# Two-layer decoder trunk: split-precision gate and numerator products, the last gate chunk by DRAM, and the order of some lanes

## The chip, the cores and the metric

The kernel runs on one core of one Trainium2 chip. The metric is the device time of one launch in microseconds (us). The kernel before took 1051.79 us in the median of three runs (1050.85 to 1053.89).

## The reference, cut to what matters

Batch 1, 256 positions (T), width 2048 (D), two layers. All weights and activations are float32.

```python
# even layer: HGRN2 (a) and RG-LRU (b) side by side
u = rmsnorm(h) @ e_w_in                     # qa, fa, ia, za, xb, zb
ya = head_rmsnorm(hgrn2(qa, fa, ia)) * silu(za)
xc = causal_conv(xb)
r  = sigmoid(einsum('bsnc,ncd->bsnd', xc, b_w_r) + b_b_r)   # 8 blocks of 128 x 128
ig = sigmoid(einsum('bsnc,ncd->bsnd', xc, b_w_i) + b_b_i)
yb = linear_scan(a(r), sqrt(1 - a*a) * ig * xc) * silu(zb)
h += concat(ya, yb) @ e_w_out
# odd layer: mLSTM, 8 heads, keys of 128, values of 256
u = rmsnorm(h) @ o_w_in                     # q, k, v, og, z, ig, fg
sc  = (q @ k.T) * weights_from_gates        # causal, so 3 of 4 blocks of 128 x 128
num = sc @ v ; den = sc.sum(-1)
yc  = head_rmsnorm(num / max(|den|, exp(-m))) * sigmoid(og) * silu(z)
h += yc @ o_w_out
# after each layer
pl = rmsnorm(p[i] @ ple_w[i]) ; h = h + sigmoid(h @ ple_gate_w[i]) * pl
return rmsnorm(h)
```

## The kernel before

**Split products.** A float32 product is made of three matmuls of a rounded type (fp32r). Each weight tile of 128 x 1024 is loaded by SP as `raw` (5 buffers), copied by ScalarE to `whi` (L131) and its remainder subtracted by VectorE into `wlo` (L132); both have four buffers, a buffer being free again once TensorE's last matmul on it is done. Activations are split the same way by `split_act` (L145, L146) into tiles `ahl` (12 buffers). `mm3` (L150 to L152) issues the three products hi-hi, hi-lo and lo-hi into one PSUM accumulator. Some smaller products are instead a float32 matmul, which the trace records as two passes: the gates of the RG-LRU (L823), the scores (L1058, L1059) and numerators (L1070, L1072) of the mLSTM, the gate sums (L929), the spread of the log weights (L265), the transposes of L542.

**Large projections.** `block` (L161: 16 matmuls of 512 columns, L167: 16 of 256) makes feature-major results, `quarter_tok` (L225, L226, L227) token-major ones: one quarter of the contraction is 24 matmuls of 512 columns, and `project_tok` makes 512 output columns of four quarters. `chunks` makes pairs of outputs in the order (0, quarters 0 to 2), (1, quarters 0 to 2), (0, 3), (1, 3), so that the last part of `y` may come later. L338 is the small per-layer embedding, L1194 to L1196 the final gate's 256-column products.

**Order.** Everything that isn't a large projection lives in generators, the lanes: `rg` (RG-LRU), `att` (HGRN2), `qk`, `mix` (mLSTM), `fm0` to `fm3` (gate output to feature-major), `emb`. `pump()` in the middle of a quarter, or between the two halves of a `block`, takes one step of some lanes, and a `yield` in a lane ends a step; so a lane's matmuls stand between two matmuls of a projection, and a `yield` more or less moves them by one pump. `drain(...)` runs a lane to its end at once. Within this, the scheduler puts each engine's instructions into one fixed order; each engine then works its list in that order and waits on semaphores for the others.

**What the change touches.** `rg_lru` holds two halves r of four blocks each: weights `bw` (128 x 1024, two gates), inputs `xc` (128 x 1024); its gates are 8 float32 matmuls per half, in two groups. `mix(j)` works on two heads: it spreads the log weights (L265), exponentiates them into `wt`, multiplies the scores by them into `scw` (L1060), and sums numerators (6 float32 matmuls per j, 257 columns: 256 values and a column of ones for the denominator); `vt` holds the values, written by ScalarE from PSUM (L1101). A `mix(j)` is started after value chunk j. `feature_major` transposes 32 x 32 blocks on VectorE, writes to DRAM through POOL's queue and reads back (`across`: one write, L507, and four reads, L510, `lag` pumps later); `feature_major_pe` does it with eight TensorE transposes of 128 x 128 (L542) for the last gate chunk (fm3), since the output projection needs it at once: `drain("fm0", ..., "fm3")` stands before `out_proj`. `gate_sums` (L929) adds four matmuls with 32 output rows per chunk c of the first layer's final gate, used for the second layer's input and forget gates.

Of the kernel before, what the change touches and what calls it, by code (L numbers as in the profile page):

```python
# [43 lines left out]
def trunk(ctx: ExitStack, tc: tile.TileContext, a, out):  # L44
# [365 lines left out]
                step(f"{lane}{kq}")  # L410
        return before

    def out_proj(hq, w, y, lane):

        act = {}
        for c in range(4):
            ps = project_tok(w, c, y)
            with tc.high_priority(offset=100):
                for hf in range(2):
                    v.tensor_tensor(out=hq[c][:, hf], in0=ps[hf], in1=hq[c][:, hf], op=ALU.add)  # L420
            start(f"{lane}{c}", to_features(hq[c], c, act, None, lane))
            step(f"{lane}{c}")
        return act
# [88 lines left out]
        for _ in range(lag):  # L512
            yield

    def feature_major(u, gain, first, y, room):

        w = room("w")
        w5 = w.rearrange("p (j c h t) -> p h c j t", j=4, c=4, h=2)
        for hf in range(2):
            v.transpose(w5[:, hf], u[:, hf].rearrange("p (c j q) -> p c j q", c=4, j=4))  # L520
        r = room("r")
        yield from across(w, r, f"du{gain}{first}", 5)
        r5 = r.rearrange("p (i c h t) -> p c h i t", i=4, c=4, h=2)
        for b in range(2):
            x = tp.tile([P, 512], F32, name="xr", tag="hn", bufs=3)
            for k in range(2):
                s.activation(x[:, k * T:(k + 1) * T].rearrange("p (h i t) -> p h i t", h=2, i=4), r5[:, 2 * b + k],
                             AF.Copy, scale=pc(gain, first + 2 * b + k))
            y[first // 2 + b] = split_act(x, "y")

    def feature_major_pe(u, gain, first, y):

        yield
        yield
        banks = []
        for b in range(2):
            ps = px.tile([P, 512], F32, name="mx", tag="mx")
            for k in range(2):
                c = (2 * b + k) * P
                for hf in range(2):  # L540
                    o = k * T + hf * P
                    te.transpose(ps[:, o:o + P], u[:, hf, c:c + P], ident)  # L542
            banks.append(ps)
        yield
        for b, ps in enumerate(banks):
            hi, lo, both = act_pair()
            for k in range(2):
                scaled_split(ps[:, k * T:(k + 1) * T], gain, first + 2 * b + k, hi[:, k], lo[:, k])
            y[first // 2 + b] = (hi, lo, both)

    def gate_tok(w, j, act, u):

# [52 lines left out]
    with m0_scope:  # L605
# [203 lines left out]
        def rg_lru(r, xc):  # L809
            bw = m0.tile([P, 2, 512], F32, name="bw", tag="bw", bufs=1)  # L810
            sy.dma_start(out=bw, in_=a["bw"][r])
            av = m0.tile([P, 1024], F32, name="av", tag="f")
            tt = m0.tile([P, 1024], F32, name="tt", tag="k")
            it = m0.tile([P, 1024], F32, name="it", tag="it", bufs=1)
            yield
            if r:
                yield
            for j in range(2):
                for w, (dst, bias) in enumerate(((av, "bbr"), (it, "bbi"))):
                    ps = px.tile([P, 512], F32, name="mx", tag="mx")  # L820
                    for i in range(2):
                        c = 2 * j + i
                        te.matmul(ps[:, i * T:(i + 1) * T], bw[:, w, c * P:(c + 1) * P], xc[:, c * T:(c + 1) * T],  # L823
                                  start=True, stop=True)
# [18 lines left out]
            v.tensor_tensor(out=it, in0=it, in1=tt, op=ALU.mult)  # L843
# [80 lines left out]
    v.tensor_tensor(out=wt[:, :, 0:16], in0=gr, in1=pall("on").unsqueeze(2).to_broadcast([P, KT, 16]), op=ALU.mult)  # L924
    gps = px.tile([P, 512], F32, name="mx", tag="mx")

    def gate_sums(c, r5):
        for x in range(4):
            te.matmul(gps[32 * x:32 * x + 32, 0:T].rearrange("p (h i t) -> p h i t", h=2, i=4), wt[:, 4 * c + x],  # L929
                      r5[:, x], start=(c == 0), stop=(c == 3))  # L930

    acth = ple_gate(hq, a["g0"], act, pls, rp0, hss0, "on", "fg", ready(act, "fe"), gate_sums)
    l0.close()
# [14 lines left out]
    with tc.tile_pool(name="m1", bufs=2) as m1:  # L948
# [89 lines left out]
        def mix(j):  # L1038
# [12 lines left out]
                s.activation(wt[:, i, T:384], wt[:, i, T:384], AF.Exp, bias=aT[:, 8 + hd:9 + hd])  # L1051
            yield
            yield
            scw = room("scw")[:, 0:768].rearrange("p (i t) -> p i t", i=2)
            for i in range(2):
                q, k = qk[j][:, i * T:(i + 1) * T], qk[4 + j][:, i * T:(i + 1) * T]
                sc = px.tile([P, 512], F32, name="mx", tag="mx")
                te.matmul(sc[:, 0:T], k[:, 0:P], q, start=True, stop=True)  # L1058
                te.matmul(sc[:, T:384], k[:, P:T], q[:, P:T], start=True, stop=True)  # L1059
                v.scalar_tensor_tensor(scw[:, i, :], sc[:, 0:384], SC, wt[:, i, :], op0=ALU.mult, op1=ALU.mult)  # L1060
            yield

            vt = vts[j]
            nm = m1.tile([P, 2, 512], F32, name="num", tag="vt", bufs=6)
            for i in range(2):
                pool, tag = ((px, "mx"), (pst, "st"))[i]
                for hf in range(2):
                    c = hf * 8 + 2 * j + i
                    ps = pool.tile([P, 512], F32, name="nu", tag=tag)[:, 0:VW]
                    te.matmul(ps, scw[:, i, hf * P:(hf + 1) * P], vt[:, 0, i], start=True, stop=(hf == 0))  # L1070
                    if hf:
                        te.matmul(ps, scw[:, i, T:384], vt[:, 1, i], start=False, stop=True)  # L1072
                    o = nm[:, hf, i * 256:(i + 1) * 256]
                    s.copy(o, ps[:, 0:256])
                    v.tensor_copy(den[:, c:c + 1], ps[:, 256:VW])
# [19 lines left out]

        for j in range(4):
            psv = project_tok(a["ov"], j, acth)
            vt = m1.tile([P, 2, 2, VW], F32, name="vt", tag="vt", bufs=6)
            gp.memset(vt[:, :, :, 256:VW], 1.0)
            for hf in range(2):  # L1100
                s.activation(vt[:, hf, :, 0:256], psv[hf].rearrange("p (i e) -> p i e", i=2), AF.Copy,  # L1101
                             scale=norm["rt"][:, hf:hf + 1])
# [19 lines left out]
        for j in range(4):  # L1122
            u = m1.tile([P, 2, 512], F32, name="u", tag="vt", bufs=6)
            gate_tok(a["oz"], j, acth, u)
            for hf in range(2):
                for i in range(2):
# [234 lines left out]
```

## Time and profile before

| | |
|---|---|
| median of three runs | 1051.79 us |
| the profiled execution | 1051.14 us |
| its span | 1049.4 us |
| TensorE (PE) busy | 1038.6 us, 99% |
| VectorE (DVE) busy | 724.3 us, 69% |
| ScalarE (ACT) busy | 594.3 us, 57% |
| GpSimd (POOL) busy | 114.4 us, 11% |
| granted TensorE clock | 0.998 |
| DMA | 225.40 MB, mean 215 GB/s |

The profile is one execution. PE's busy time counts overlapped instructions once. Matmuls are pipelined: the "mean ns of one" in a group of matmuls is from its start to its modelled end and overlaps with the next one's, so the cost of one in a stream is read from the chain of waits, whose pieces give a start and the time until the next piece starts. Where a piece says "x8", 8 records lie in it; a float32 matmul leaves two records.

### The profile page before, as it was taken

To read this page: it belongs to the slowest core of one execution; us is meant where nothing else is said; L and a number is where in the kernel's file an instruction comes from. 1 tells how busy PE (TensorE), PEld (TensorE's weight loads), DVE (VectorE), ACT (ScalarE), POOL (GpSimd) and SP (SyncE) were. 2 spreads that over 40 slices of the span, in tenths; PEclk is the share of its full clock that TensorE was granted. 3 is DMA by queue.
4 is the path that set the end of the run, shared out by engine and by line. 5 is a ranking of instruction groups with operands and counts; after the bars stand their busy time and mean duration, and the time that the engine had idled before them with its cause. 6 is when DMAs were issued, how large, how long until landed. Compare 5 with 4: busy or idle time off the path is not lost.

```text
span 1049.4 us, 14961 instructions
## 1 busy us (share of the span) xinstructions
PE 1038.6 (99%) x5504; PEld 869.1 (83%) x5504; DVE 724.3 (69%) x1085; ACT 594.3 (57%) x893; POOL 114.4 (11%) x162
## 2 busy tenths in 40 slices
PE   9999999999999999999999999999999999999996
PEld 7888888888888888887888788888888888888886
DVE  6857897997877666766569864454457767666675
ACT  7775545869654444565557765544445565444553
POOL 0001232522201111111021000000001110111000
PEclk9999999999999999999999999999999999999999
DMA  9865544545867877687597644446557775977652
GB/s 350 311 205 192 172 164 157 182 150 192 275 234 258 249 247 230 212 277 235 177 271 248 203 169 160 161 161 201 199 188 225 250 262 187 294 239 242 201 181 81
DMA packets 64587, 225.40 MB, mean 215 GB/s; under 512 B 8065, under 2 KB 9345, under 8 KB 64513
## 3 DMA queue, kind: packets, MB, share of 16 engines
q1 hardware_dynamic: 55440, 196.38, 56.5%
q0 software_dynamic: 8496, 27.27, 8.6%
q8 instruction: 43, 0.70, 0.3%
q10 hardware_dynamic: 576, 0.79, 0.2%
q14 instruction: 32, 0.25, 0.1%
HBM read 211.30 MB, written 13.11 MB: 214 GB/s over the span
## 4 chain that ended last, share of the span: by engine, by line
PE 97%; DMA 1%; ACT 1%; DVE 0%; issue 0%; SPq 0%; ACTq 0%
PE mm L225 22%; PE mm L226 22%; PE mm L227 22%; PE mm L161 11%; PE mm L167 6%; PE mx L225 2%; PE mx L227 2%; PE mx L226 2%; PE mm L338 1%; DMA xq<-in_xT_dram 1%; PE mm L1196 1%; PE mm L1195 1%; PE mm L1194 1%; PE mx L823 1%; PE nu L1070 1%; PE mx L661 0%
## 5 line engine op out<-in xcount | busy, mean ns | idle before, releaser
L132 DVE TENSOR_TENSOR wlo<-raw,whi 128x1024 fp32r<-128x1024 f32 (+1 forms) x364 | 439.9, 1220 | 246.4 <-ACT whi L131 211.3
L131 ACT CAST whi<-raw 128x1024 fp32r<-128x1024 f32 (+1 forms) x364 | 378.3, 1043 | 356.4 <-PE mm L227 254.8
L225 PE MATMUL mm<-whi,ahl 128*128 128x512 f32 x1024 | 401.5, 392 | 0.0
L227 PE MATMUL mm<-whi,ahl 128*128 128x512 f32 x1024 | 398.5, 389 | 0.0
L226 PE MATMUL mm<-wlo,ahl 128*128 128x512 f32 x1024 | 398.4, 389 | 0.0
L225 PEld LDWEIGHTS mm<-whi,ahl 128*128 128x128 f32 x1024 | 192.2, 188 | 42.0 <-issue 2.1
L227 PEld LDWEIGHTS mm<-whi,ahl 128*128 128x128 f32 x1024 | 192.2, 188 | 40.5
L226 PEld LDWEIGHTS mm<-wlo,ahl 128*128 128x128 f32 x1024 | 192.3, 188 | 39.8 <-DVE wlo L132 0.5
L161 PE MATMUL mm<-ahl,whi 128*128 128x512 f32 x512 | 122.1, 390 | 0.0
L161 PEld LDWEIGHTS mm<-ahl,whi 128*128 128x128 f32 x512 | 94.2, 188 | 18.3
L167 PE MATMUL mm<-ahl,wlo 128*128 128x256 f32 x512 | 67.7, 285 | 0.0
L167 PEld LDWEIGHTS mm<-ahl,wlo 128*128 128x128 f32 x512 | 64.9, 191 | 2.2
L225 PE MATMUL mx<-whi,ahl 128*128 128x512 f32 x96 | 37.5, 391 | 0.0
L227 PE MATMUL mx<-whi,ahl 128*128 128x512 f32 x96 | 37.4, 389 | 0.0
L226 PE MATMUL mx<-wlo,ahl 128*128 128x512 f32 x96 | 37.3, 389 | 0.0
L507 POOL DMA_DIRECT2D ducn<-w x3 | 1.7, 561 | 206.2 <-DVE w L520 206.2
L173 ACT COPY sm<-mm 128x256 f32<-128x256 f32 x32 | 11.7, 366 | 19.1 <-PE mm L167 19.0
L225 PEld LDWEIGHTS mx<-whi,ahl 128*128 128x128 f32 x96 | 18.0, 188 | 3.7
L227 PEld LDWEIGHTS mx<-whi,ahl 128*128 128x128 f32 x96 | 18.0, 188 | 3.8
L226 PEld LDWEIGHTS mx<-wlo,ahl 128*128 128x128 f32 x96 | 18.0, 188 | 3.7
L971 DVE SCALAR_TENSOR_TENSOR qk<-xr,prm,qk 128x255 f32<-128x255 f32 (+2 forms) x48 | 20.4, 475 | 0.6 <-ACT qk L968 0.5
L1195 PE MATMUL mm<-wlo,ahl 128*128 128x256 f32 x64 | 18.1, 283 | 0.0
(304 smaller groups left out, 877.3 us busy)
## 6 DMA issues: line engine op xcount, KB each, us to landing
raw<-in_ew_dram SPq DMA_DIRECT2D x64, 512.0 KB, 4.4
raw<-in_g_dram SPq DMA_DIRECT2D x56, 512.0 KB, 4.7
raw<-in_eo_dram SPq DMA_DIRECT2D x32, 512.0 KB, 4.8
raw<-in_oqk_dram SPq DMA_DIRECT2D x32, 512.0 KB, 4.6
raw<-in_ov_dram SPq DMA_DIRECT2D x32, 512.0 KB, 3.8
raw<-in_oog_dram SPq DMA_DIRECT2D x32, 512.0 KB, 3.7
raw<-in_oz_dram SPq DMA_DIRECT2D x32, 512.0 KB, 4.2
raw<-in_oo_dram SPq DMA_DIRECT2D x32, 512.0 KB, 4.5
```

The lines of the kernel that those rows point to most:

```text
L131: last["act"] = s.copy(h, r).ins
L132: last["dve"] = v.tensor_tensor(out=l, in0=r, in1=h.bitcast(F32), op=ALU.subtract).ins
L161: last["pe"] = te.matmul(ps, parts[k // 8][0][:, c:c + P], act[k // 2][2][:, (k % 2) * 512:(k % 2 + 1) * 512], start=(k == 0), stop=False).ins
L167: last["pe"] = te.matmul(ps[:, T:2 * T], parts[k // 8][1][:, c:c + P], act[k // 2][0][:, k % 2], start=False, stop=(k == KT - 1)).ins
L173: s.copy(small, ps[:, T:2 * T])
L225: te.matmul(ps[hf], xh, wh, start=(k == 0), stop=False)
L226: te.matmul(ps[hf], xh, wl, start=False, stop=False)
L227: last["pe"] = te.matmul(ps[hf], xl, wh, start=False, stop=(k == KT - 1)).ins
L338: last["pe"] = te.matmul(ps[hf], tokens(pact[x], k, hf), (hi, lo)[y][:, k * 512:(k + 1) * 512], start=(n == mine[0]), stop=(n == mine[-1]) ...
L823: te.matmul(ps[:, i * T:(i + 1) * T], bw[:, w, c * P:(c + 1) * P], xc[:, c * T:(c + 1) * T], start=True, stop=True)
L971: v.scalar_tensor_tensor(dst[:, sh:T], pi[:, 0:T - sh], pc("ccw", k * 16 + n), dst[:, sh:T], op0=ALU.mult, op1=ALU.add)
L1195: te.matmul(ps[hf], xh, wl, start=False, stop=False)
```

## The change

It has six edits.

1. The RG-LRU's gates become three products each. `bw` is split into a `whi` and a `wlo` buffer of the weights' own pools, `xc` into two `ahl` tiles. One step is added ahead of the gates.
2. The numerators become three products each. The scores are written over `wt`, split into `sh` and `sl`; the values' remainder `vl` is an `ahl` tile. The value tile has 258 columns instead of 257.
3. The last gate chunk goes by VectorE transposes and DRAM like the other three; `feature_major_pe` is gone. `out_proj` takes its chunks from a generator, and the second one draws from `chunks` and waits for the `fm` lanes as it needs them.
4. The first layer's mixer outputs (`fm` of "an") start their transposes one step later, with a lag of 4 instead of 5.
5. All four `mix(j)` are started behind value chunk 0, each waits for its keys and values by steps, and the step after the numerators is gone, so that the next pair's spread stands right behind them.
6. `gate_sums` collects two chunks and issues eight matmuls at once, twice instead of four groups of four.

```diff
-    def out_proj(hq, w, y, lane):
+    def out_proj(hq, parts, lane):
         act = {}
-        for c in range(4):
-            ps = project_tok(w, c, y)
+        for c, ps in enumerate(parts):
...
-    def feature_major(u, gain, first, y, room):
-
+    def feature_major(u, gain, first, y, room, lag):
+
+        if lag < 5:
+            yield
         w = room("w")
         w5 = w.rearrange("p (j c h t) -> p h c j t", j=4, c=4, h=2)
         for hf in range(2):
             v.transpose(w5[:, hf], u[:, hf].rearrange("p (c j q) -> p c j q", c=4, j=4))
         r = room("r")
-        yield from across(w, r, f"du{gain}{first}", 5)
+        yield from across(w, r, f"du{gain}{first}", lag)
...
-    def feature_major_pe(u, gain, first, y):
-
-        yield
-        yield
-        banks = []
-        for b in range(2):
-            ps = px.tile([P, 512], F32, name="mx", tag="mx")
-            for k in range(2):
-                c = (2 * b + k) * P
-                for hf in range(2):
-                    o = k * T + hf * P
-                    te.transpose(ps[:, o:o + P], u[:, hf, c:c + P], ident)
-            banks.append(ps)
...
@@ rg_lru
             yield
             if r:
                 yield
+            bh, bl = (wp.tile([P, 2, 512], F32R, name=n, tag=n) for n in ("whi", "wlo"))
+            s.copy(bh, bw)
+            v.tensor_tensor(out=bl, in0=bw, in1=bh.bitcast(F32), op=ALU.subtract)
+            xs = [split_act(xc[:, j * 512:(j + 1) * 512], "xc") for j in range(2)]
+            yield
             for j in range(2):
                 for w, (dst, bias) in enumerate(((av, "bbr"), (it, "bbi"))):
                     ps = px.tile([P, 512], F32, name="mx", tag="mx")
                     for i in range(2):
                         c = 2 * j + i
-                        te.matmul(ps[:, i * T:(i + 1) * T], bw[:, w, c * P:(c + 1) * P], xc[:, c * T:(c + 1) * T],
-                                  start=True, stop=True)
+                        mm3(ps[:, i * T:(i + 1) * T], bh[:, w, c * P:(c + 1) * P], bl[:, w, c * P:(c + 1) * P], xs[j], i,
+                            True, True)
...
-                start(f"fm{g}", feature_major(u, "an", 4 * g, y, room0))
+                start(f"fm{g}", feature_major(u, "an", 4 * g, y, room0, 4))
...
-    act = out_proj(hq, a["eo"], y, "fe")
+    act = out_proj(hq, (project_tok(a["eo"], c, y) for c in range(4)), "fe")
...
+    held5 = []
+
     def gate_sums(c, r5):
-        for x in range(4):
-            te.matmul(gps[32 * x:32 * x + 32, 0:T].rearrange("p (h i t) -> p h i t", h=2, i=4), wt[:, 4 * c + x],
-                      r5[:, x], start=(c == 0), stop=(c == 3))
+        held5.append((c, r5))
+        if c % 2 == 0:
+            return
+        for n, r in held5:
+            for x in range(4):
+                te.matmul(gps[32 * x:32 * x + 32, 0:T].rearrange("p (h i t) -> p h i t", h=2, i=4), wt[:, 4 * n + x],
+                          r[:, x], start=(n == 0), stop=(n == 3))
+        held5.clear()
...
-        VW = 257
+        VW = 258
...
@@ mix(j)
             yield
             yield
-            scw = room("scw")[:, 0:768].rearrange("p (i t) -> p i t", i=2)
+            while 4 + j not in qk:
+                yield
             for i in range(2):
...
-                v.scalar_tensor_tensor(scw[:, i, :], sc[:, 0:384], SC, wt[:, i, :], op0=ALU.mult, op1=ALU.mult)
-            yield
-
-            vt = vts[j]
+                v.scalar_tensor_tensor(wt[:, i, :], sc[:, 0:384], SC, wt[:, i, :], op0=ALU.mult, op1=ALU.mult)
+            sh, sl = (bp.tile([P, 1024], F32R, name=n, tag="wt")[:, 0:768].rearrange("p (i t) -> p i t", i=2)
+                      for n in ("sh", "sl"))
+            s.copy(sh, wt)
+            v.tensor_tensor(out=sl, in0=wt, in1=sh.bitcast(F32), op=ALU.subtract)
+            yield
+
+            while len(vts) <= j:
+                yield
+            vh, vl = vts[j]
...
-                    te.matmul(ps, scw[:, i, hf * P:(hf + 1) * P], vt[:, 0, i], start=True, stop=(hf == 0))
-                    if hf:
-                        te.matmul(ps, scw[:, i, T:384], vt[:, 1, i], start=False, stop=True)
+                    for b, o in ((0, hf * P), (1, T))[:1 + hf]:
+                        for x, y, n in ((sh, vh, VW), (sl, vh, VW), (sh, vl, T)):
+                            te.matmul(ps[:, 0:n], x[:, i, o:o + P], y[:, b, i], start=(b == 0 and x is sh and y is vh),
+                                      stop=(b == hf and y is vl))
...
             nums[j] = nm
-            yield
...
         for j in range(4):
             psv = project_tok(a["ov"], j, acth)
-            vt = m1.tile([P, 2, 2, VW], F32, name="vt", tag="vt", bufs=6)
-            gp.memset(vt[:, :, :, 256:VW], 1.0)
+            vt = m1.tile([P, 2, 2, VW], F32R, name="vt", tag="vt", bufs=6)
+            gp.memset(vt.bitcast(F32)[:, :, :, 256:VW], 1.0)
+            vl = ap.tile([P, 1024], F32R, name="vl", tag="ahl").rearrange("p (h i e) -> p h i e", h=2, i=2)
             for hf in range(2):
...
+                v.scalar_tensor_tensor(vl[:, hf], src, norm["rt"][:, hf:hf + 1], vt[:, hf, :, 0:256].bitcast(F32),
+                                       op0=ALU.mult, op1=ALU.subtract)
+            vts.append((vt, vl))
+            if j == 0:
+                drain("qk0", "qk2")
+                for c in range(4):
+                    start("mix", mix(c))
+                start("mix", mix_norm())
-            vts.append(vt)
-            for c in (j // 2, 2 + j // 2):
-                drain(f"qk{c}")
-            start("mix", mix(j))
-        start("mix", mix_norm())
...
-            start(f"fm{j}", feature_major(u, "cn", 4 * j, y, room) if j < 3 else feature_major_pe(u, "cn", 4 * j, y))
+            start(f"fm{j}", feature_major(u, "cn", 4 * j, y, room, 5))
...
-        drain("fm0", "fm1", "fm2", "fm3")
+        step("fm3")
         start("emb", embed_norm())
-        act = out_proj(hq, a["oo"], y, "fo")
+        act = out_proj(hq, chunks(a["oo"], 4, y, ready(y, "fm")), "fo")
```

What it does to the order, first on TensorE around the numerators of a head pair (nu; L1070 and L1072 before, L1072 in the changed file). Before:

```order
L226 MATMUL mm<-wlo,ahl 128x512
L227 MATMUL mm<-whi,ahl 128x512
L1070 MATMUL nu<-vt,scw 128x257 x2
L1072 MATMUL nu<-vt,scw 128x257
L1070 MATMUL nu<-vt,scw 128x257 x2
L1072 MATMUL nu<-vt,scw 128x257
L225 MATMUL mm<-whi,ahl 128x512
```

In the change, the end of the same group:

```order
L1072 MATMUL nu<-vl,sh 128x256
L1072 MATMUL nu<-vt,sh 128x258
L1072 MATMUL nu<-vt,sl 128x258
L1072 MATMUL nu<-vl,sh 128x256
L265 MATMUL mx<-s_5670,identr 128x256 x2
L225 MATMUL mm<-whi,ahl 128x512
```

A group of 6 matmuls (12 recorded passes) becomes one of 18, and the next pair's spread (L265, of the split log weights s), which came one pump of 24 matmuls later before, stands right behind it.

On ScalarE, around the gates of the second RG-LRU half (av and it are the gates' sigmoids, o the HGRN2 output copied from PSUM, sq its squares, u a gate chunk). Before:

```order
L827 ACTIVATE av<-mx,prm 128x256 x2
L827 ACTIVATE it<-mx,prm 128x256 x2
L131 CAST whi<-raw 128x1024 x2
L556 ACTIVATE u<-mm,rth 128x512
L833 ACTIVATE tt<-av,sp_235 128x256 x2
L834 ACT_TABLE_LOAD
L834 ACTIVATE av<-av,spm_236 128x256
L787 COPY o<-mx 128x512
L790 ACTIVATE sq,hss<-mx 128x128 x4
L787 COPY o<-mx 128x512
L790 ACTIVATE sq,hss<-mx 128x128 x4
L827 ACT_TABLE_LOAD
```

In the change:

```order
L800 CAST whi<-bw 128x1024
L145 CAST ahl<-xc 128x2x256
L131 CAST whi<-raw 128x1024
L537 ACTIVATE u<-mm,rth 128x512
L768 COPY o<-mx 128x512
L771 ACTIVATE sq,hss<-mx 128x128 x4
L768 COPY o<-mx 128x512
L771 ACTIVATE sq,hss<-mx 128x128 x4
L131 CAST whi<-raw 128x1024 x2
L813 ACT_TABLE_LOAD
L813 ACTIVATE av<-mx,prm 128x256 x2
```

The copy of bw into a `whi` buffer (L800) and the second split of xc (L145) are added, and the first sigmoids have moved behind the squares. Before, both weight copies of the coming quarter (L131 x2) stood ahead of the squares; now one does, and the other is the first of the two behind them.

On VectorE at the same place, in the change:

```order
L801 TENSOR_TENSOR wlo<-bw,whi 128x1024
L132 TENSOR_TENSOR wlo<-raw,whi 128x1024
L538 SCALAR_TENSOR_TENSOR u<-u,mm 128x512
L146 TENSOR_TENSOR ahl<-xc,ahl 128x2x256
L872 TENSOR_TENSOR u<-u,o 128x512
L772 TENSOR_SCALAR hss<-hss 128x8
L232 TENSOR_SCALAR hnt<-hss 128x8
L234 TENSOR_SCALAR hny<-hss 128x8
L233 TENSOR_SCALAR hnr<-hnt 128x8
L236 TENSOR_TENSOR hnt<-hnr 128x8
L237 TENSOR_TENSOR hnt<-hnt,hny 128x8
L238 SCALAR_TENSOR_TENSOR hnr<-hnt,hnr 128x8
L132 TENSOR_TENSOR wlo<-raw,whi 128x1024
```

The subtraction for `bl` (L801), the remainder of xc (L146) and seven small operations of the reciprocal root on 128x8 stand ahead of the weights' subtraction L132 in the last row; before, both weight subtractions of that quarter stood ahead of all the small ones, between the operations on the two halves of u.

More of the change, by code (lines that the diff above doesn't have):

```diff
@@ L529, in feature_major @@
             y[first // 2 + b] = split_act(x, "y")
-    def feature_major_pe(u, gain, first, y):
-        yield
-        yield
-        banks = []
-        for b in range(2):
-            ps = px.tile([P, 512], F32, name="mx", tag="mx")
-            for k in range(2):
-                c = (2 * b + k) * P
-                for hf in range(2):
-                    o = k * T + hf * P
-                    te.transpose(ps[:, o:o + P], u[:, hf, c:c + P], ident)
-            banks.append(ps)
-        yield
[L545 to L549, printed above, removed]
     def gate_tok(w, j, act, u):
@@ L1069, in mix @@
                     ps = pool.tile([P, 512], F32, name="nu", tag=tag)[:, 0:VW]
-                    te.matmul(ps, scw[:, i, hf * P:(hf + 1) * P], vt[:, 0, i], start=True, stop=(hf == 0))
-                    if hf:
-                        te.matmul(ps, scw[:, i, T:384], vt[:, 1, i], start=False, stop=True)
+                    for b, o in ((0, hf * P), (1, T))[:1 + hf]:
+                        for x, y, n in ((sh, vh, VW), (sl, vh, VW), (sh, vl, T)):
+                            te.matmul(ps[:, 0:n], x[:, i, o:o + P], y[:, b, i], start=(b == 0 and x is sh and y is vh),
+                                      stop=(b == hf and y is vl))
                     o = nm[:, hf, i * 256:(i + 1) * 256]
                     s.copy(o, ps[:, 0:256])
-                    v.tensor_copy(den[:, c:c + 1], ps[:, 256:VW])
+                    v.tensor_copy(den[:, c:c + 1], ps[:, 256:257])
                     sq = tp.tile([P, 512], F32, name="sq", tag="sq")[:, 0:256]
@@ L1097, in trunk @@
             psv = project_tok(a["ov"], j, acth)
-            vt = m1.tile([P, 2, 2, VW], F32, name="vt", tag="vt", bufs=6)
-            gp.memset(vt[:, :, :, 256:VW], 1.0)
+            vt = m1.tile([P, 2, 2, VW], F32R, name="vt", tag="vt", bufs=6)
+            gp.memset(vt.bitcast(F32)[:, :, :, 256:VW], 1.0)
+            vl = ap.tile([P, 1024], F32R, name="vl", tag="ahl").rearrange("p (h i e) -> p h i e", h=2, i=2)
             for hf in range(2):
-                s.activation(vt[:, hf, :, 0:256], psv[hf].rearrange("p (i e) -> p i e", i=2), AF.Copy,
-                             scale=norm["rt"][:, hf:hf + 1])
-            vts.append(vt)
-            for c in (j // 2, 2 + j // 2):
-                drain(f"qk{c}")
-            start("mix", mix(j))
-        start("mix", mix_norm())
+                src = psv[hf].rearrange("p (i e) -> p i e", i=2)
+                s.activation(vt[:, hf, :, 0:256], src, AF.Copy, scale=norm["rt"][:, hf:hf + 1])
+                v.scalar_tensor_tensor(vl[:, hf], src, norm["rt"][:, hf:hf + 1], vt[:, hf, :, 0:256].bitcast(F32),
[6 more added lines that the diff above has]
+                start("mix", mix_norm())
         y = {}
```

## The prediction

> **What bounds the kernel now.** I read three views of the profile first: busy time by engine, the clock by slices, and what TensorE waited for.
>
> ```profile
> PE 1038.6 (99%) x5504; PEld 869.1 (83%) x5504; DVE 724.3 (69%) x1085; ACT 594.3 (57%) x893; POOL 114.4 (11%) x162
> PEclk9999999999999999999999999999999999999999
> PE 97%; DMA 1%; ACT 1%; DVE 0%; issue 0%; SPq 0%; ACTq 0%
> PE st L95 <- POOL ones L90: 1.1, 1, 1.1
> PE mm L338 <- DVE wlo L132: 0.6, 1, 0.6
> ```
>
> TensorE is busy 99% of the span at the full clock in every slice; the chain of waits is TensorE's for 97%. Its only waits on other engines are 1.1 and 0.6 us, both in the first microseconds. So a microsecond of TensorE work less is a microsecond of span less, and a microsecond by which a split comes late is one more. Nothing else counts unless TensorE is made to wait. VectorE has most to do where the RG-LRU runs, below, and there the change adds to it.
>
> The profiled run took 1051.14 us with a span of 1049.4, so 1.74 us lie around the span; the median of the runs is 0.65 us above it. I make the sum against 1051.14 and add 0.65.
>
> **Gates.** The chain of waits has the four groups of 8 records, and beside them a stream of products of the new kind, 256 columns, each with weights of its own:
>
> ```profile
> 192.34 1.92 PE mx L823 x8
> 194.27 1.91 PE mm L167 x16
> 199.83 1.73 PE mx L823 x8
> 231.57 1.73 PE mx L823 x8
> 241.45 1.73 PE mx L823 x8
> ```
>
> Removed: 1.92 + 3 x 1.73 = 7.11 us for 16 float32 matmuls in 32 passes, 0.216 us a pass. Added: 48 products at 1.91/16 = 0.119 us, 5.73 us. Difference -1.38.
>
> The Trainium skill ("TensorE: Matmul & The Clock Gate", section "LDWEIGHTS (loading the stationary operand)") gives a weight load the number of columns over 1.2 in nanoseconds, about 107 ns for 128 columns, and says that in a stream the two kinds set the spacing together. It speaks against the change if the loads aren't hidden: gates and numerators would issue 120 products instead of 80 passes, and by that figure the 40 further loads would cost an estimated 4.3 us, which would leave about nothing. The stream above doesn't show it: 0.119 us with a load each.
>
> **Numerators.** One head pair of four:
>
> ```profile
> 616.16 0.87 PE nu L1070 x4
> 617.02 0.43 PE nu L1072 x2
> ...
> 618.76 0.23 PE mm L225
> ```
>
> 12 passes take 618.76 - 616.16 = 2.60 us and the next matmul is not slowed. In their place stand 18 products at 0.119 to 0.121 us (two thirds have 258 columns, 2 in 256 more), 2.16 us: -0.44 a pair, -1.76 in all. No row has an fp32r product of 258 columns. Its lower bound is 0.119; for an upper one I take the step of the 512-column products (0.23 in the last row), if an odd width were to cost a whole bank row: 48 x 0.11 = +5.3 us. I take the row beside it in width, 256 columns.
>
> **Last gate chunk and gate sums.**
>
> ```profile
> 858.75 0.44 PE mx L542 x4
> 864.69 0.44 PE mx L542 x4
> 467.04 0.23 PE mm L227
> 467.26 0.57 PE mx L929 x8
> 467.83 0.43 PE mm L225
> ```
>
> The eight transposes go: -0.88 us. A gate-sum group costs 0.57 plus the next matmul's 0.43 - 0.23 = 0.20 above its usual step: 0.77. There were four. Two with twice the records save the two entries and exits: what isn't its eight passes. I estimate a pass by a quarter of the 0.216 us of a 128-column weight's (a group writes 32 rows of 128), 8 x 0.054 = 0.43, so 0.34 a group; -0.68. Bounds: nothing (the exit comes with the eight records), or 2 x 0.77 = -1.54 (the joined records overlap wholly).
>
> Moving the spread behind the numerators leaves its matmuls and its exit as they are:
>
> ```profile
> 624.25 0.43 PE mx L265 x2
> 624.67 0.43 PE mm L225
> ```
>
> The exit of 0.20 stays with any projection matmul that follows; the entry may be shared. Three of them, 0 to -0.3; I take 0. Moving the mixer transposes adds no TensorE work and comes well ahead of the first `out_proj`; 0.
>
> TensorE's work: -1.38 - 1.76 - 0.88 - 0.68 = -4.7 us.
>
> **What the splits add, and whether TensorE waits.** Added to VectorE: per RG-LRU half one subtraction of 128x1024 and two of 128x512; per head pair one of 128x768 and two of 128x512. To ScalarE the copies of the same shapes. The rows for these shapes and the place where VectorE is fullest:
>
> ```profile
> 178.00:226.00 48.00, 48.00 (x460) 40.69 (x459) 46.03 (x71) 33.64 (x50) 23.56 (x15) 1.00 0.49 164
> 218.60 1.23 DVE L843 TENSOR_TENSOR it<-it,tt 128x1024 f32<-128x1024 f32 x1
> 219.75 3.21 DVE L132 TENSOR_TENSOR wlo<-raw,whi 128x1024 fp32r<-128x1024 f32 x2
> 233.72 0.69 DVE L557 SCALAR_TENSOR_TENSOR u<-u,mm 128x512 f32<-128x512 f32 x1
> 228.00 1.06 ACT L131 CAST whi<-raw 128x1024 fp32r<-128x1024 f32 x1 [0.30 <-PE mm L227]
> 223.94 0.39 PE L226 MATMUL mm<-wlo,ahl 128*128 128x512 f32 x1
> ```
>
> First half (r=0): 1.23 + 2 x 0.69 = 2.6 us more on a VectorE that is busy 46.03 of 48 us there. The splits run ahead, though. The tightest pair ends at 219.75 + 3.21 = 222.96, and TensorE's first product with its second tile starts at 223.94: 0.98 us of slack before. In the new order the RG-LRU's own operations (the 1.23 us one ahead of this pair among them) have moved behind it. I count again by the rows: the pair would be ready some 2 us early, and the next pair, around 228 us, 0 to 0.9 us early. Late here is 0 to 0.5 us; I take 0.2.
>
> Second half (r=1): here a `whi` buffer is held by `bw`, one weight copy waits behind the squares, and its subtraction behind seven small operations.
>
> ```profile
> 238.77 1.11 PE mx L783 x10
> 240.28 0.57 ACT L787 COPY o<-mx 128x512 f32<-128x512 f32 x1
> 241.75 0.61 ACT L787 COPY o<-mx 128x512 f32<-128x512 f32 x1
> 243.14 0.27 ACT L790 ACTIVATION_READ_ACCUMULATOR sq<-mx 128x1 f32 x1
> 243.44 0.17 DVE L791 TENSOR_SCALAR hss<-hss 128x8 f32<-128x8 f32 x1 [2.93 <-ACT sq L790]
> 244.46 0.17 DVE L238 SCALAR_TENSOR_TENSOR hnr<-hnt,hnr 128x8 f32<-128x8 f32 x1
> ```
>
> From the start of the 12 small matmuls (24 passes at 0.11, 2.6 us): ScalarE copies the first bank at 0.9; copy and four squares take 241.75 - 240.28 = 1.47 us, the second bank's 1.66; done at 2.7 + 1.7 = 4.4. The weight copy (1.06) is done at 5.4; the small operations come at a pace of 0.2 from 4.5 on, seven of them to 5.9, and the subtraction (1.22) ends at 7.1. TensorE is at the product that needs it after 2.6 + 18 x 0.23 = 6.7. So it waits 0.4 us; queued behind on VectorE is only the next pair's subtraction, whose use is 18 matmuls and a group of gates away, so nothing else is late. Bounds: nothing, or 1.5 if ScalarE starts late by its 1.06 us copy of `bw`.
>
> Head pairs:
>
> ```profile
> 610.77 1.02 DVE L1060 SCALAR_TENSOR_TENSOR scw<-mx,wt 128x384 f32<-128x384 f32 x2
> ```
>
> A score group is 4 passes of 256 columns and 4 of 128, by the 0.216 above 1.3 us; then come these two products, a copy and a subtraction of 128x768 (at most 1.06 and 1.23 by the rows for 1024). That is some 4.6 us from the pump, and 1.3 us and 24 matmuls (5.5 us) of TensorE lie ahead of the use: no wait. Only in the fourth pair the remainder of its values, made behind two weight subtractions, comes within 0.1 us of its use: 0.1, and up to 1.2 if one more such subtraction gets ahead.
>
> The DRAM way of the last gate chunk lies beside at least six quarters of the output projection (6 x 24 x 0.23 = 33 us) by the order that `chunks` makes:
>
> ```profile
> 837.03 0.56 POOL L507 DMA_DIRECT2D ducn<-w  x1 [15.87 <-DVE w L520]
> 840.92 2.18 POOL L510 DMA_DIRECT2D r<-ducn  x4 [3.33 <-DMA ducn<-w]
> 843.09 1.11 POOL L367 DMA_DIRECT2D row<-in_rows_dram  x2
> r<-ducn POOLq DMA_DIRECT2D x12, 128.0 KB, 5.8
> row<-in_rows_dram POOLq DMA_DIRECT2D x6, 512.0 KB, 8.8
> ```
>
> Write to last landing is 3.9 + 2.2 + 5.8 = 12 us, to which two ScalarE/VectorE splits of some 3 us come: 15 us, hidden in 33. Queued behind its five issues on POOL are the row loads of the embedding's gains, issued before at 843.1, now after the fourth chunk. That chunk is whole at about 858 us, its write would be issued at 859.4, its reads from 863 to 865.2, the rows land 8.8 later at 874.5; VectorE multiplies by them (L1151, L1155 in the change) ahead of a weight subtraction that TensorE wants 121 matmuls after the embedding's start, at 853.1 + 121 x 0.228 = 880.7. VectorE stands for 2 us and the subtraction is ready at 877: 3.7 us to spare. I cost it at nothing; if reads and rows took twice their times, 14.6 us more, TensorE would wait 10.9.
>
> Waits: 0.2 + 0.4 + 0.1 = 0.7. **Sum**: -4.7 + 0.7 = -4.0: 1047.1 for a run like the profiled one, 1047.8 beside the median.
>
> **The rivals.**
> A. Passes saved, few waits: 1047.8. For it: no wait on TensorE in a kernel at 99%; all prices from the same kernel's stream.
> B. The splits come late in several places, 1 to 3 us in all, each by a chain like the one at 243 us. For: 46.03 of 48 us busy, 0.98 us of slack. Against: the new order puts the weight subtractions first. 1051.79 - 4.7 + 2.5 = 1049.6: within 0.3%.
>
> C. The other side. One of four `whi`/`wlo` buffers is held by `bw` from its copy to its last gate product, twice, over two or three quarters of 5.5 us. A weight split can then start only when a pair of buffers comes free, and if copy, subtraction and what stands ahead of them take longer than the 18 matmuls left (4.1 us), every split of that stretch is late by the excess. Six splits a half, each late by the mean of the 0.4 counted above and its bound of 1.5, 0.9: 12 x 0.9 = 10.8, 1051.79 - 4.7 + 10.8 = 1057.9. It is slower than before from an excess of 0.4 each. For: one is late by my own count. Against: only that one stands behind the squares; the others have about 1 us by the same count.
>
> D. The 258-column products step like those of 512: 1047.8 + 5.3 = 1053.1, within 0.3%. For it no row; against it the L167 stream at half that width.
>
> E. The weight loads aren't hidden where weights change with each short product. No row has a load alone; by the pass of 128 columns (0.11, eight in 0.88) 40 more would cost 4.4: 1052.2. Against it the same stream, 0.119 with a load each. The page named above has the rule for it.
>
> F. The last gate chunk's detour, or the row loads behind it, take twice their times: 1047.8 + 10.9 = 1058.7. For: both lie on one queue, beside weight loads. Against: 3.7 us to spare.
>
> **How the numbers follow.** Chances: A 0.60, B 0.20, C 0.08, D 0.05, E 0.03, F 0.04. A's own range is 1045.9 (nothing late, gate sums and spreads at their better bounds: -0.7 - 0.9 - 0.3) to 1049.6 (the longest of the waits at its upper bound, +1.1, and the gate sums' gain gone, +0.7). From there it reaches to 1051.9, no change, over B: 8 in 10. The bound that tells faster or slower from no change is 0.3% here, 3.16 us: 1048.6 and 1054.9. A lies below 1048.6 for all but 0.04; B above it but for 0.02; D and E are within; C and F beyond. Faster 0.58, same 0.30, slower 0.12.
>
> **What would show it.** The chain of waits should have groups of 12 products from L150 to L152 at 1.4 to 1.5 us, 18 of L1072 at 2.1 to 2.2, no L542, two gate-sum groups of some 1.0 us. TensorE's busy time should be 4 to 5 us less. Its list of waits should have one on `wlo` of L132 near 243 us of 0.4 us or less and hardly another. I am wrong if that list holds a microsecond or more on `wlo`, on the split scores or on `y`, or if the products of L1072 step at more than 0.13 us.

## The result, and the profile after

| | before | after |
|---|---|---|
| first comparison, median | 1051.36 us (1050.85 to 1053.89, 6 runs) | 1045.6 us (1045.06 to 1046.3, 6 runs) |
| its ratio | | 0.994 (0.9927 to 0.9952) |
| both again, later, median | 1050.67 us (15 runs) | 1045.4 us (5 runs) |
| its ratio | | 0.9955 (0.9942 to 0.9967) |
| span of the profiled execution | 1049.4 us | 1043.7 us |

By these medians the change makes the kernel faster by 5.3 to 5.8 us, 0.5 to 0.55%. The forecast was 4.0 us, and 1045.6 lies 0.3 us below the forecast range.

The page of the changed kernel, busy times and the chain by engine; then its list of what TensorE waited for:

```profile
PE 1033.8 (99%) x5536; PEld 868.9 (83%) x5536; DVE 736.3 (71%) x1103; ACT 598.6 (57%) x903; POOL 113.3 (11%) x167
PE 98%; DMA 1%; ACT 0%; SPq 0%; DVE 0%; issue 0%; ACTq 0%
```

```profile
PE st L95 <- POOL ones L90: 1.1, 1, 1.1
PE mm L338 <- DVE wlo L132: 0.4, 1, 0.4
```

Both waits lie in the first microseconds, as before. TensorE is still the bound, with 4.8 us less work; VectorE has 12 us more. The chain of waits has the new groups as forecast:

```profile
204.58 0.82 PE mx L642 x64
205.39 0.32 PE mx L150
205.71 0.12 PE mx L151
...
614.03 2.14 PE nu L1072 x18
616.17 0.43 PE mx L265 x2
616.60 0.43 PE mm L225
...
849.03 10.88 PE mm L338 x48
```

18 numerator products take 2.14 us, a product of 258 columns steps like one of 256, and the 48 products of the embedding run through without transposes between them. The first two rows correct a term of the sum: after 64 products with 32 output rows (L642) the next matmul takes 0.20 us more, here the first gate product (0.32). In the profile of before the same 0.20 was in the 1.92 that the prediction counted as a gate group, so one term was 0.19 too large.

To see where the time went, each matmul on a weight tile in the trace of before is set beside the same one in the trace of after; there are 4672 in both. The span then falls into three parts: up to number 100 of them (counted from 0), from there to the last matmul (the middle), and the tail.

| trace | to number 100 | middle | tail |
|---|---|---|---|
| before | 29.56 | 1010.69 | 9.10 |
| before again (e5) | 28.67 | 1010.52 | 9.10 |
| after | 29.03 | 1005.94 | 8.69 |
| after again (e9) | 28.98 | 1005.97 | 8.68 |

The middle is 4.6 to 4.7 us shorter, in both traces of each. By place: gates -1.14 and a wait of 0.19 beside them, gate sums -0.66, numerators and spreads -1.98, last gate chunk -0.99; together -4.6, and 0.15 at the embedding that one trace of before has and the other has not. The start scatters by 0.9 us between two traces of one kernel, so the 0.5 us by which it differs here can be put down to no edit. The tail is 0.42 shorter, of which more below.

### The profile page after: what moved, and what is told of

Its sections match the earlier page's. It is cut to its first block, busy times and chain, and to the rows that moved or that the text cites. A ratio compares the mean times of both kernels' runs of the same rounds, so it can differ in the third digit from the quotient of the medians.

```text
span 1043.7 us, 15070 instructions
## 1 busy us (share of the span) xinstructions
PE 1033.8 (99%) x5536; PEld 868.9 (83%) x5536; DVE 736.3 (71%) x1103; ACT 598.6 (57%) x903; POOL 113.3 (11%) x167
## 4 chain that ended last, share of the span: by engine, by line
PE 98%; DMA 1%; ACT 0%; SPq 0%; DVE 0%; issue 0%; ACTq 0%
PE mm L225 22%; PE mm L226 22%; PE mm L227 22%; PE mm L161 11%; PE mm L167 6%; PE mx L227 3%; PE mx L225 3%; PE mx L226 3%; PE mm L338 2%; PE nu L1072 1%; PE mm L1200 1%; PE mm L1199 1%; PE mm L1198 1%; DMA raw<-in_pw_dram 1%; PE mx L642 0%; PE mx L764 0%
## 5 line engine op out<-in xcount | busy, mean ns | idle before, releaser
L132 DVE TENSOR_TENSOR wlo<-raw,whi 128x1024 fp32r<-128x1024 f32 (+1 forms) x364 | 438.0, 1215 | 235.6 <-ACT whi L131 202.4
L131 ACT CAST whi<-raw 128x1024 fp32r<-128x1024 f32 (+1 forms) x364 | 378.4, 1043 | 335.9 <-PE mm L227 232.5
L225 PE MATMUL mm<-whi,ahl 128*128 128x512 f32 x992 | 387.7, 391 | 0.0
L226 PE MATMUL mm<-wlo,ahl 128*128 128x512 f32 x992 | 386.1, 389 | 0.0
L227 PE MATMUL mm<-whi,ahl 128*128 128x512 f32 x992 | 385.9, 389 | 0.0
L225 PEld LDWEIGHTS mm<-whi,ahl 128*128 128x128 f32 x992 | 186.3, 188 | 39.9 <-issue 1.2
L227 PEld LDWEIGHTS mm<-whi,ahl 128*128 128x128 f32 x992 | 186.2, 188 | 39.1
L226 PEld LDWEIGHTS mm<-wlo,ahl 128*128 128x128 f32 x992 | 186.3, 188 | 38.5 <-DVE wlo L132 0.5
L225 PE MATMUL mx<-whi,ahl 128*128 128x512 f32 x128 | 50.0, 391 | 0.0
L227 PE MATMUL mx<-whi,ahl 128*128 128x512 f32 x128 | 49.8, 389 | 0.0
L226 PE MATMUL mx<-wlo,ahl 128*128 128x512 f32 x128 | 49.8, 389 | 0.0
L227 PEld LDWEIGHTS mx<-whi,ahl 128*128 128x128 f32 x128 | 24.0, 188 | 5.0
L226 PEld LDWEIGHTS mx<-wlo,ahl 128*128 128x128 f32 x128 | 24.0, 188 | 5.0
L225 PEld LDWEIGHTS mx<-whi,ahl 128*128 128x128 f32 x128 | 24.0, 188 | 4.9
```

The costliest lines, as they stand in the source:

```text
L131: last["act"] = s.copy(h, r).ins
L132: last["dve"] = v.tensor_tensor(out=l, in0=r, in1=h.bitcast(F32), op=ALU.subtract).ins
L225: te.matmul(ps[hf], xh, wh, start=(k == 0), stop=False)
L226: te.matmul(ps[hf], xh, wl, start=False, stop=False)
L227: last["pe"] = te.matmul(ps[hf], xl, wh, start=False, stop=(k == KT - 1)).ins
```

## The experiments

In what follows "middle" is this part of the span; two traces of one kernel agree in it within 0.03 us (after) and 0.17 us (before), where the times of the runs tell about a microsecond. Each experiment below has one trace.

**Each edit alone.** e1 has only the gates, on the kernel before:

```diff
+            bh, bl = (wp.tile([P, 2, 512], F32R, name=n, tag=n) for n in ("whi", "wlo"))
+            s.copy(bh, bw)
+            v.tensor_tensor(out=bl, in0=bw, in1=bh.bitcast(F32), op=ALU.subtract)
+            xs = [split_act(xc[:, j * 512:(j + 1) * 512], "xc") for j in range(2)]
+            yield
...
-                        te.matmul(ps[:, i * T:(i + 1) * T], bw[:, w, c * P:(c + 1) * P], xc[:, c * T:(c + 1) * T],
+                        mm3(ps[:, i * T:(i + 1) * T], bh[:, w, c * P:(c + 1) * P], bl[:, w, c * P:(c + 1) * P], xs[j], i,
```

> The kernel before with the first edit alone, three-product gates. Theory (the change's gain is TensorE's passes in the middle of the program; the 0.98 us that the traces differ in at the start and in the tail are scatter of single executions): four groups of float32 passes at 1.72 us become four of twelve products at 1.43 to 1.45, with one wait of about 0.2 us on the weights' low part in the second half: -0.9 to -1.2 us, and start and tail differ from the profile of before by some tenths either way. Rival (the ends belong to the change): a part of the 0.98 us at the ends comes with one of the edits; if with this one, -1.9 us.

Measured: 1050.55 us, ratio 1.0002 (0.9993 to 1.0011); middle 1010.79, 0.2 us more than the mean of before's two. The gates are 1.14 us shorter here too, and a wait took it back:

```profile
PE mm L226 <- DVE wlo L132: 1.1, 1, 1.1
```

It stands at the product that the prediction had worked out, in the second half near 243 us, but is 1.35 us in all by the steps beside it, not 0.2. The theory's number for this run fell. The timeline of VectorE in this run shows what is late:

```profile
239.82 0.68 DVE L891 TENSOR_TENSOR u<-u,o 128x512 f32<-128x512 f32 x1
240.42 1.29 DVE L520 STREAM_TRANSPOSE wu<-u 128x512 f32<-128x512 f32 x2
241.64 0.13 DVE L791 TENSOR_SCALAR hss<-hss 128x8 f32<-128x8 f32 x1
...
242.61 0.17 DVE L238 SCALAR_TENSOR_TENSOR hnr<-hnt,hnr 128x8 f32<-128x8 f32 x1
242.70 1.22 DVE L132 TENSOR_TENSOR wlo<-raw,whi 128x1024 fp32r<-128x1024 f32 x1
```

And the same place in the changed kernel:

```profile
239.88 0.69 DVE L872 TENSOR_TENSOR u<-u,o 128x512 f32<-128x512 f32 x1
240.48 0.17 DVE L772 TENSOR_SCALAR hss<-hss 128x8 f32<-128x8 f32 x1
...
241.49 0.17 DVE L238 SCALAR_TENSOR_TENSOR hnr<-hnt,hnr 128x8 f32<-128x8 f32 x1
241.58 1.22 DVE L132 TENSOR_TENSOR wlo<-raw,whi 128x1024 fp32r<-128x1024 f32 x1
242.71 0.16 DVE L236 TENSOR_TENSOR hnt<-hnr 128x8 f32<-128x8 f32 x1
242.79 0.70 DVE L521 STREAM_TRANSPOSE wu<-u 128x512 f32<-128x512 f32 x1
```

Two transposes of the mixer's output (L520, 1.2 us) stand ahead of the small operations in e1 and behind the weights' subtraction in the changed kernel. The fourth edit, the later mixer transposes, does that.

e2 has edits 2 and 5 (numerators and the mixer lane), e3 edits 3 and 4 (last gate chunk by DRAM, generator of chunks, later mixer transposes), e4 edit 6 (gate sums), each as in the diff above, on the kernel before.

> The kernel before with the second and the fifth edit, three-product numerators and the mixer lane's new order. Theory: four groups fall from 2.61 to 2.15 us, and the spread behind the numerators saves up to 0.06 each: -1.9 to -2.1 us, no wait on TensorE. Rival: with the ends -2.9 us.

Measured: 1048.42 us, ratio 0.9984 (0.9975 to 0.9992); middle 1008.55, -2.05. No new wait on TensorE in the middle.

> The kernel before with the last gate chunk by DRAM, the output projection drawing its chunks from a generator, and the later mixer transposes (third and fourth edit). Theory: eight transposes less, -1.0 to -1.2 us (two groups of 0.49, the rest a short wait at the embedding that may or may not come), nothing else. Rival of the prediction: the detour or the row loads behind it come late, +1 us or more beside the -1.1. Rival on the ends: -2.0 us.

Measured: 1049.0 us, ratio 0.9987 (0.9978 to 0.9997); middle 1009.52, -1.1. No wait at the chunk or at the row loads: the detour by DRAM is hidden.

> The kernel before with the sixth edit alone, gate sums of two chunks at once. Theory: -0.66 us, 0.33 for each of the two groups joined, hardly to be told from no change by the times, but in the trace at the two places. Rival on the ends: -1.6 us.

Measured: 1049.65 us, ratio 0.9994 (0.9985 to 1.0003), not to be told from no change; middle 1010.01, -0.6: -0.67 at the two places, and beside the second trace of before a wait of 0.16 elsewhere, at a projection.

The middles of e1 to e4 add up to +0.2 - 2.05 - 1.1 - 0.6 = -3.55. The change has -4.65. The missing 1.1 us point to an interplay: the gates need the later transposes. The next two runs ask for it.

**Undone and done in pairs.** e10 is the changed kernel with the fourth edit taken back:

```diff
-                start(f"fm{g}", feature_major(u, "an", 4 * g, y, room0, 4))
+                start(f"fm{g}", feature_major(u, "an", 4 * g, y, room0, 5))
```

> The changed kernel without its fourth edit: the mixer's transposes at their old place. Theory (the later transposes keep 1.2 us of VectorE's time out of a stretch in which VectorE is never idle and the gates add 2.6 us): the wait at the weights' low part near 242 us grows from 0.2 to 1.3 us, +1.1 us in the middle against the change. Rival (as the prediction had it, the fourth edit is worth nothing for TensorE): no difference to the change.

Measured: 1046.65 us against 1045.4 for the change beside it; middle 1007.15, +1.2. The wait is back:

```profile
PE mm L226 <- DVE wlo L132: 1.1, 1, 1.1
```

e11 is the kernel before with the first and the fourth edit alone, the gates of e1 and the line with 4.

> The kernel before with the first and the fourth edit only: three-product gates and the later mixer transposes. Theory: -0.9 to -1.0 us in the middle against the kernel before, where the gates alone gave +0.1 to +0.3; the wait near 242 us is 0.2. Rival (the gates need the other edits as well): the wait stays above 1 us.

Measured: 1049.55 us, ratio 0.9992 (0.9983 to 1.0001); middle 1009.93, -0.7; at the gates -1.14 and a wait of 0.19, as in the change, and a wait of 0.34 at a product of the embedding, where the first trace of before has 0.15 and its second none; what makes it stays open. With e11 in place of e1 the parts sum to -4.4 (the later transposes are in it and in e3, where they do nothing). Set beside the second trace of before, without this 0.34 and the 0.16 of e4, they sum to -4.57, which is what the change has beside that trace. So the interplay is settled: without the fourth edit the first is worth nothing.

**How full VectorE is.** e8 issues the subtraction for `bl` twice in each half of the RG-LRU in the changed kernel:

```diff
             v.tensor_tensor(out=bl, in0=bw, in1=bh.bitcast(F32), op=ALU.subtract)
+            v.tensor_tensor(out=bl, in0=bw, in1=bh.bitcast(F32), op=ALU.subtract)
```

> The changed kernel with the subtraction for the gate weights' low part issued twice in each half, 1.2 us more of VectorE's time each. Theory (the splits have slack, the prediction's waits were too large): nothing in the first half; in the second at most a few tenths. Rival (VectorE full, its waits near): the weights come late by about 1.2 us in each half, +1 to +2.4 us.

Measured: 1049.68 us, the runs between 1048.17 and 1050.75, the trace of one at 1048.72; middle 1008.93, +3.0 against the change, of which 2.24 at the same product and the rest in four waits of 0.1 to 0.3 before it. The two subtractions are 2.3 us of it (2 x 1.14 as they follow one another); the other 0.7 us came in the first half's stretch, where one operation on VectorE (L694) took 1.78 us instead of 0.41, and why it did stays open. So 2.24 is not simply the two subtractions, but an addition some 40 us earlier did reach the late product. The rival is right on the stretch, though not in each half by itself. Busy times by stretch say why; first the kernel before, then the changed one, the columns are length, then busy time of PE, its weight loads, VectorE, ScalarE and GpSimd:

```profile
185.00:243.00 58.00, 58.00 (x514) 49.42 (x512) 53.13 (x78) 45.76 (x81) 20.38 (x15) 1.00 0.53 178
185.00:243.00 58.00, 58.00 (x522) 49.31 (x522) 57.14 (x91) 45.58 (x80) 16.08 (x14) 1.00 0.48 164
```

The change fills VectorE from 53.13 to 57.14 of 58 us up to the late subtraction. Work added ahead of it there makes that one wait longer (e8), and work moved behind it makes it shorter (e10, e11). The weights in between are late by 0.1 to 0.3 us only in e8; the order has them ahead of the RG-LRU's work, which passes the delay on.

**The held buffer.** e6 takes the parts of the gate weights out of the weights' buffers in the changed kernel; `bh` gets a buffer of its own and `bl` one of the activations':

```diff
-            bh, bl = (wp.tile([P, 2, 512], F32R, name=n, tag=n) for n in ("whi", "wlo"))
+            bh = m0.tile([P, 2, 512], F32R, name="bh", tag="bh", bufs=1)
+            bl = ap.tile([P, 1024], F32R, name="bl", tag="ahl").rearrange("p (w c) -> p w c", w=2)
```

> The changed kernel, with the parts of the gate weights in a tile of their own and in an activation buffer, so that they hold none of the four weight buffers. Theory: the held buffer is what pushed one weight copy behind the squares; it stands ahead of them again, the wait of 0.19 us in the second half is gone, and the trace saves 0.2 us more in the middle than the change does. Rival: VectorE's own work there (2.6 us more a half) makes it late: the wait stays.

Measured: 1051.34 us, ratio to before 1.0008 (0.9999 to 1.0017), so some 6 us slower than the change; middle 1011.48. The wait of 0.19 is gone, as expected, and a larger one has come at another place:

```profile
PE mx L714 <- DVE f L720: 3.6, 1, 3.6
```

With the buffers free the scheduler placed other work of the RG-LRU first, and VectorE reached an operation of the HGRN2 lane (L720) at 222.87 us that it starts at 214.72 in the changed kernel. Since e6 changed the order as well as the buffers, it doesn't price the held buffer by itself; in the changed kernel that can be no more than the wait of 0.19. What it shows is that on a full VectorE the order decides who is late.

**Two further versions.** e7 issues all gate sums in one group (`if c < 3: return` in place of `if c % 2 == 0`), e12 does that and moves one product of the first RG-LRU half to GpSimd:

```diff
-            v.tensor_tensor(out=it, in0=it, in1=xc, op=ALU.mult)
+            (v if r else gp).tensor_tensor(out=it, in0=it, in1=xc, op=ALU.mult)
```

> The changed kernel with the gate sums of all four chunks in one group of sixteen. Theory: an entry and exit cost 0.33 us whatever the group's size: 0.3 us less in the trace than the change at that place. Rival: a chunk's tile held for two more chunks holds up the next one: a wait on TensorE there.

Measured: 1044.94 us against 1050.51 for the kernel before, ratio 0.9947 (0.9933 to 0.996); middle 1005.50, -0.45 against the change (0.3 was expected), no wait. In its chain the group stands as

```profile
514.95 0.23 PE mm L227
515.18 1.86 PE mx L921 x32
517.04 0.43 PE mm L225
```

Its median is the lowest of all kernels here; against the change the times alone don't tell it, the trace does.

> The changed kernel with the gate sums once in one group of sixteen, and one product of the first RG-LRU half (128x1024, 1.2 us on VectorE) on GpSimd. Theory (VectorE is never idle up to the late weights): besides the -0.45 of the sums the wait of 0.2 us near 242 us is gone, -0.6 us in the middle against the change. Rival: GpSimd, which takes some 2.6 us for it, hands its next product late to TensorE, and a wait of 1 us or more comes there.

Measured: 1045.9 us; middle 1006.53, +0.6 against the change. The wait near 242 us is gone, and others of 0.27 and 0.77 us came on the weights' low parts at 226.7 and 233.9 us: the scheduler ordered the stretch anew, and GpSimd, which took 2.40 us for the product, began its next one for TensorE 2 us later. The expected gain didn't come; of the two causes neither was taken away alone.

**The same kernels again.**

> The kernel before once more, unchanged, for another trace of it. Theory (ends are scatter): start (first projection matmul of the first quarter) and tail differ from the first profile by some tenths of a microsecond, and the ratio is 1.000. Rival (the ends belong to the change): start and tail repeat the first profile within 0.1 us.

Measured: 1050.84 us against 1050.51, ratio 1.0003 (0.9994 to 1.0012). The start differs by 0.9 us, the tail by nothing, so the theory held for the start and the rival for the tail.

> The changed kernel once more, unchanged, on the chip of the next three runs. Both theories: the middle of the program (from the 100th projection matmul to the last) takes 1005.9 us again within 0.1; the difference in time to the kernel before is -4.8 (the middle) -0.4 (the tail), so -5.2 us, and the start adds some tenths of scatter; no instruction packet in the tail.

Measured: 1045.4 us against 1050.67; middle 1005.97, tail 8.68. The sum of the parts, -4.65 - 0.42, is -5.1, and the times of the runs say -5.27.

## Why the prediction was wrong

- **The bound** was read rightly. Every microsecond of TensorE's work saved came out of the span, and none of the signs named for being wrong came: the mechanism, rival A, held, and sizes in it were off.
- **The passes** were sized well in the sum, -4.7 against -4.8 in the trace (-1.14, -1.98, -0.99, -0.66), and in part by luck. The gates' saving was put 0.24 too high, mostly by the exit of the 32-row products counted in the first group; the spreads, taken at 0, and the transposes' exits made it good.
- **The step that failed is "Waits: 0.2 + 0.4 + 0.1 = 0.7".** The trace has one wait, at the product that was worked out, of 0.19:

```profile
242.55 0.39 PE L225 MATMUL mm<-whi,ahl 128*128 128x512 f32 x1
242.85 0.50 PE L226 MATMUL mm<-wlo,ahl 128*128 128x512 f32 x1
243.19 0.40 PE L227 MATMUL mm<-whi,ahl 128*128 128x512 f32 x1
```

The late subtraction (241.58 and 1.22 us in the rows above) ends at 242.80, L226 starts 0.05 us later, and the two steps from L225 to L227 take 0.30 and 0.34 us where a step is 0.23. The reckoning for the second half holds to 0.2 us: the small operations begin 4.6 us after the first of the 12 small matmuls (4.5 in the reckoning), but take 1.1 us instead of 1.4, since some of them follow after 0.1 us and not 0.2 (240.48 to 241.58 in the rows above). The other two waits don't exist.
- **What the prediction didn't see: the tail**, 0.42 us. The sum has no term for it; its instructions are the same in both kernels.
- **The rest of the miss** is scatter and the reference. Between the two profiled runs, 1051.14 and 1045.46, lie 5.7 us instead of 4.0. Of the 1.7 us more, 0.5 are the waits, 0.4 the tail, 0.5 the start, 0.15 the embedding and 0.1 the passes. The median was put 0.65 above the profiled run and lay 0.14 above it. The reference moved too: the median of before was 1051.36 beside the changed kernel, not 1051.79, and 1050.45 to 1050.84 in later groups of 11 to 33 runs.
- **Also wrong, though it cost nothing in the sum: "Moving the mixer transposes adds no TensorE work ...; 0".** It adds none, but it takes 1.2 us off VectorE ahead of the one late subtraction. e10 shows it is worth 1.2 us. My count at that place used the new order, and so had it without naming it.
- **Rivals.** B was half right: the stretch is full (57.14 of 58 us, e8), but the order keeps all weights but one ahead of it. C fell: one split is late by 0.19 us, not six in each half by 0.9; e6, which frees the buffer, doesn't test it alone. D and E fell with the 2.14 us of 18 products. F fell with e3.
- **The range** was too narrow at its lower end: it had "nothing late" there and no room for ends that differ. The tail's 0.42 us alone are more than the 0.3 by which 1045.6 lies below it.

## What to carry to other kernels

Where one engine is busy 99%, sum its instructions from the steps in the chain of waits, and look for the exit cost of a narrow group in the piece behind it. Where a second engine is full for tens of microseconds, don't ask what an added operation costs but which consumer stands last in that stretch: in e8 most of what was added early arrived there, 2.24 of 3.0 us. An edit that only moves work out of such a stretch can be worth as much as the one that saves passes, and edits tried one by one can then look worthless (e1, 1.0002).

## What the runs showed of the hardware

**A tail that is 0.42 us longer with a late instruction packet.** The DMA view of the last nine microseconds of the kernel before has a packet that the changed kernel's has not:

```profile
q14 instruction: 1, 0.01, 0.3%
```

The three traces with such a packet there (before, e5, e4) have tails of 9.10 to 9.12 us, the eleven without 8.67 to 8.69, whatever was edited. In the three it comes 1.2 us after the last operation on a tile, and the end of the program 0.42 us later than in the others. It doesn't go by the count of instructions alone: the page of e3 has 14958 and no such packet, that of e4 14960 and one. That loading a piece of the program there costs the 0.42 us is argued from these fourteen, not tested by itself.

**A halved clock after 3.6 us of idling.** In e6 TensorE stood still for 3.6 us, up to 223.60; the columns are as above, the granted clock stands behind the five busy times:

```profile
220.00:223.50 3.50, 0.00 (x0) 0.00 (x0) 3.50 (x6) 1.11 (x2) 0.00 (x0) 1.00 0.37 122
224.50:226.00 1.50, 1.50 (x15) 1.20 (x6) 1.49 (x3) 0.14 (x1) 1.17 (x1) 0.50 0.57 232
```

```profile
225.40 0.43 PE mm L227
225.82 0.43 PE mm L225
```

Products of 512 columns took 0.43 instead of 0.23 us until about 226.9 (the granted clock is 0.59 from 226.5 to 227.0 and 1.00 behind it), which added 1.2 us or so to the wait itself. The 2.2 us of waiting in e8, up to 246.14, left the clock at 1.00:

```profile
246.00:250.00 4.00, 3.86 (x23) 3.42 (x24) 3.50 (x12) 1.57 (x4) 0.93 (x2) 1.00 0.59 160
```

The Trainium skill ("TensorE: Matmul & The Clock Gate", section "HAM oscillation — how this bites in real kernels") warns of idle gaps above about 3.4 us; both runs agree.
